# Pace of a woven-in matrix inverse: seven steps instead of six per ten filler calls, then its sixteen transfers at sixteen per ten

## The chip, the cores and the metric

One core of one Trainium2 chip runs the whole kernel. The metric is device microseconds of one execution; lower is better. Five engines matter here: TensorE (PE, with its weight loads PEld), VectorE (DVE), ScalarE (ACT), GpSimd (POOL) and SyncE (SP). Each executes its own list of instructions in order and waits on semaphores of the others. SP, ACT and POOL also issue DMA transfers from their lists.

## The reference

One decoder layer on x of 1024 tokens by 1024 channels, all in fp32:

- h = RMSNorm(x), and one projection P = h W_in whose columns go to three branches and to the branch gates.
- Branch A, RWKV-7 time mixing, 8 heads of 64: a state S (64x64 per head) follows S = S*w + (S(-kk))(kk*a)^T + v k^T over the tokens, and y = S r is normalised per head.
- Branch B, stick-breaking attention, 8 heads of 64: strictly causal, attn = sigmoid(z) times the running product of (1 - sigmoid(z)) between key and query.
- Branch M, attention into 256 memory tokens, 4 heads of 128: softmax(q k^T) v with normalised q and k.
- x += (sum over branches of sigmoid(G_b) * (branch_b W_br[b])) W_out, then x += ConvFFN(RMSNorm(x)).

The recurrence of branch A is computed in chunks of 64 tokens. For 8 heads and 16 chunks that needs the inverses of 128 triangular 64x64 matrices, which are worked out one after the other column, for all 128 at once.

## The kernel before

**Number format.** Every fp32 operand of a large matmul is split into a high and a low part; three matmuls (high-high, low-high, high-low) make one product. For a weight block ACT makes the high part (L80, `wh`) and POOL the low part (L81, `wl`), from a raw tile that SP loads (L76, `wr`). PE (L115) runs the products.

**Stages around the change.** `run` builds one list of *items*, the filler: projections, gate projections (`gate_item`) and the memory keys and values, each a generator that does about an eighth of its matmuls per call. Against this filler, `weave` advances a main generator: first `rwkv_prep` for four head pairs, then the first attention `sb_attn` (64 units), then the second attention `mem_attn` (8 units), then the recurrence `stage2`. After every step of the main generator it calls the filler so many times (1.03 per step in the first attention, 1.6 in the second).

**The inverse.** `inverse` holds the 128 matrices in one tile `inst`, a matrix to a partition. For each of 62 columns it does two DVE instructions over s*(63-s) elements, a product into a scratch tile `it` (L474) and a sum into `inst` (L476). Then the diagonal is set (L478), and sixteen DMAs on POOL's queue (L483) store the result to DRAM as `td`, which `stage2` reads back (L515). Each of the 124 DVE instructions and each of the sixteen transfers is one step. The steps are pulled by the filler: `pumped` adds `pace[0]` to a counter at each call and pulls one step per ten.

```python
def pumped():
    due = 0
    for _ in self.stream(items):
        due += pace[0]
        while due >= 10:
            due -= 10
            next(inv, None)
        yield
```

The pace is zero until the first attention begins. Whatever is left of the inverse is drained ahead of the last gates before `stage2`.

**First attention, one unit:** scores on PE, sigmoid on ACT (L842, into `at`), the running product on DVE (L848, a scan over up to 1024 elements), two units later the transposes on PE (L105), their copy on ACT (L860), and the products with v.

**Second attention, one unit:** `front` makes the scores on PE into `g` banks; DVE takes the row maximum (L1058, `mxt`) and scales it (L1061, `nb`); ACT does four exponentials from the banks (L1064); DVE takes reciprocals and scales (L1068, L1070). Two units later `mid` transposes on PE, and ACT copies out (L1079). Four units later `back` multiplies by v, ACT copies (L1089) and stores (L1090).

**Filler next to it:** a memory query projection ends in `fin` (L1026, L1027 on ACT, L1028 on DVE), which empties its two `mm` banks. A gate projection ends with two copies on ACT (L749), a product on DVE (L750), a sigmoid on ACT (L753) and a store (L755). PSUM has four banks named `mm` and four named `g`; a matmul that starts a bank waits for the reader of what stood there.

**Who sets the order.** Matmuls and instructions marked with `pinned` or `ordered` keep the order in which they are written. For the others (most of ACT, much of DVE, POOL and SP) a scheduler chooses the place from its own estimate of when things are ready, so that a step that is moved changes the order of instructions that it has nothing to do with.

Of the kernel before, what the change touches and what calls it, by code (L numbers as in the profile page):

```python
# [49 lines left out]
class Trunk:  # L50
# [1710 lines left out]
    def run(self):  # L1761
        nc, tc = self.nc, self.tc
        self.setup()
        sx, sw, sl, sr = ExitStack(), ExitStack(), ExitStack(), ExitStack()
        self.pool_x = sx.enter_context(tc.tile_pool(name="xp", bufs=1))
        self.pool_a = sr.enter_context(tc.tile_pool(name="ap", bufs=1, side="right"))
        self.bufs_w = {"w4": 3, "A": 4, "qk": 8, "at": 7, "ys": 1, "it": 1}
        self.pc = [self.pool_a.tile([128, NC], F32, name=f"pc{p}") for p in range(4)]
        self.inst = self.pool_a.tile([128, 64, 64], F32, name="inst", tag="inst")
        self.stored, self.open_gates = set(), []  # L1770
        drain = lambda g: [None for _ in g]
        chain = itertools.chain
        self.pool_w = sw.enter_context(tc.tile_pool(name="w1", bufs=1, side="right"))
        krv, qk, mq = ([[] for _ in range(4)] for _ in range(3))
        krv[0].append(self.startup())
        self.pin = True
        marks, self.fresh = {"k0"}, []
        self.marks = marks
        items = [self.shift_item(i + p, krv[p], f"{n}{p}") for p in range(4) for n, i in (("k", 4), ("r", 0), ("v", 8)) if (p, n) != (0, "k")]
        items += self.sb_v()  # L1780
        self.v = []
        zero = self.t4("ys", n=512)
        nc.vector.memset(zero[0:1], 0.0)
        nc.sync.dma_start(self.vsd[0:1], zero[0:1])
        inv = self.inverse()
        gq = [(b, d) for b in (1, 0) for d in range(8)]
        gq[14:14] = [(2, 0), (2, 1)]
        self.stored = set(gq)
        gate = lambda hook={}: self.gate_item(*gq.pop(0), hook)
        mark = lambda name: lambda: marks.add(name)  # L1790
        for p in range(4):
            kp, kss, qp, hooks = self.sb_qk(p, qk[p])
            items += [*([self.differ] if p == 0 else []), kp, gate({6: self.spread_last} if p == 0 else {}), kss, qp, gate(hooks), mark(f"sb{p}")]
        prep, mss, mv, mk = self.mem_kv()
        mqi = [None] * 4
        for h in range(4):
            mqi[h] = self.mem_q(h, mq[h], {2: mqi[h - 1][1], 4: mark(f"mq{h - 1}")} if h > 1 else {})
        items += [gate({0: prep}), gate(), gate({2: prep}), lambda: mss(0), mv[0], lambda: mss(1), *mv[1:], *mk, mqi[0][0], mark("kv")]
        items += [self.mem_kss, gate({1: mqi[0][1]}), self.mem_kbc, mqi[1][0], mark("mq0")]
        items += [mqi[2][0], mqi[3][0], gate({2: mqi[3][1], 4: mark("mq3")}), gate(), mark("mem")]  # L1800
        ld1, hk1, br1 = self.branch(1, True)
        ld2, hk2, br2 = self.branch(2, False)
        items += [lambda: drain(inv), gate(), ld1, gate(hk1), mark("y1"), *br1, ld2, gate(hk2), *br2, gate()]
        assert not gq
        pace = [0]
# [10 lines that stand above are left out]
        pump = pumped()  # L1816

        def need(name):
            while name not in marks:
                next(pump)  # L1820

        for p in range(4):
            self.weave(self.rwkv_prep(p, krv[p], need), pump, 1.0)
        pace[0] = 6
        need("sb0")
        self.weave(self.sb_attn(qk, need), pump, 1.03, 0)
        need("kv")
        self.weave(self.mem_attn(mq, need), pump, 1.6, 0)
        need("mem")
        st2 = self.stage2()  # L1830
        next(st2)
        need("y1")
        self.weave(st2, pump, 2.15, 0)
        self.weave(self.group_norm(), pump, 1, 0)
        drain(pump)
        self.close_gates()
        self.pin = False
        sx.close()
        self.pool_l = sl.enter_context(tc.tile_pool(name="l4", bufs=16))
        self.branch_last()  # L1840
        sums = self.out_proj()
        self.pool_a.tile([128, 56], F32, name="pad_a")
        sw.close()
        self.bufs_r = {"u": 3, "p1": 2}
        self.pool_r = sr.enter_context(tc.tile_pool(name="ff", bufs=2, side="right", reuse_waits="tile"))
        self.up_phase(*sums)
        self.pool_r.tile([128, 40], F32, name="pad_r", bufs=1)
        self.down_phase()
        sr.close()
        sl.close()  # L1850
# [67 lines left out]
```

## Time and profile before

| what | value |
|---|---|
| time, median of 3 runs | 1827.49 us (1827.40 to 1828.59) |
| the profiled execution's own time | 1825.74 us |
| its span, first to last instruction | 1824.0 us |
| PE busy | 1785.2 us (98%) |
| DVE, ACT, POOL busy | 1182.7, 866.2, 789.8 us |
| first inverse step, last inverse step, last of the sixteen transfers (starts) | 293.9, 687.1, 742.7 us |
| first attention (first scan to last scan) | 332.0 to 626.9 us |

The profile names a tile without its number, and a line can be that of a helper: almost every matmul is L115. A timeline row gives start, duration, engine, line, operation, output<-inputs, size, how many equal instructions are merged, and in brackets the idle time of the engine before it with what ended it. A row of the chain of waits gives start, duration, and engine, tile and line. A windows row gives the stretch, then busy time and number of instructions for each engine, then PEclk (the TensorE clock that was granted, as a share of full speed) and the DMA share.

### The profile page before, as it was taken

The page shows a single profiled execution, that of the slowest core. Times are in us where ns is not written, and L with a number is a line of the kernel's source. Part 1 is how long each engine was busy: PE and PEld are TensorE (multiplying, and loading weights), DVE is VectorE, ACT ScalarE, POOL GpSimd, SP SyncE. Part 2 cuts the span into 40 slices and gives each one's busy share as a digit, 9 for nine tenths or more (in the row PEclk, how much of TensorE's full clock was granted, in tenths as well). Part 3 has the DMA queues.
Part 4 walks back from the last instruction along what each step waited for, and adds up shares of the span by engine and source line. Part 5 has one row for each costly group of instructions (what it writes and reads, how often), then busy time and mean ns, then how long its engine had stood idle before and what let it go on. Part 6 is the DMA issues. An engine that isn't in the chain of part 4 may idle for free.

```text
span 1824.0 us, 27302 instructions
## 1 busy us (share of the span) xinstructions
PE 1785.2 (98%) x10468; PEld 1444.6 (79%) x10468; DVE 1182.7 (65%) x1622; ACT 866.2 (47%) x1553; POOL 789.8 (43%) x447
## 2 busy tenths in 40 slices
PE   8999999999999999899999999989999999999999
PEld 6777778888787887677777878868888888888877
DVE  5667674787888854234542892487776777794595
ACT  5544344556566635434544333554544445444343
POOL 2323353322231433212323541587767777545454
PEclk9999999999999999899999999999999999999999
DMA  4255564211112323468754562322322323395475
GB/s 183 70 163 183 181 218 157 73 41 44 53 56 87 115 92 94 128 236 288 252 181 156 180 233 98 121 86 89 120 98 87 121 93 121 112 347 194 138 259 179
DMA packets 122341, 261.29 MB, mean 143 GB/s; under 512 B 28506, under 2 KB 43098, under 8 KB 122083
## 3 DMA queue, kind: packets, MB, share of 16 engines
q1 hardware_dynamic: 84738, 193.71, 32.3%
q10 hardware_dynamic: 33696, 53.23, 8.0%
q0 software_dynamic: 3776, 12.62, 2.3%
q8 instruction: 82, 1.34, 0.3%
q14 instruction: 49, 0.39, 0.1%
HBM read 178.99 MB, written 80.48 MB: 142 GB/s over the span
## 4 chain that ended last, share of the span: by engine, by line
PE 71%; DVE 3%; issue 3%; ACT 2%; POOL 2%; DMA 2%; SPq 0%; ACTq 0%; POOLq 0%; DVEq 0%
PE mm L115 58%; PE g L115 10%; PE g L105 3%; POOL dw L1657 1%; DVE at L1208 1%; DMA A<-yd 1%; DVE mg L1215 0%; DVE at L1207 0%; DVE w L750 0%; DVE inst L476 0%; DMA u<-in_w_down_dram 0%; DMA mrd<-w 0%; DMA x<-in_x_dram 0%; ACT w L753 0%; DMA wr<-in_w_out_dram 0%
## 5 line engine op out<-in xcount | busy, mean ns | idle before, releaser
L81 POOL TENSOR_TENSOR wl<-wr,wh 128x1024 fp32r<-128x1024 f32 x77 | 198.9, 2584 | 504.0 <-ACT wh L80 504.0
L115 PE MATMUL mm<-xhi,wh 128*128 128x512 f32 x784 | 262.2, 415 | 8.7 <-ACT xhi L185 7.8
L115 PE MATMUL mm<-xlo,wh 128*128 128x512 f32 x784 | 245.1, 394 | 0.9 <-DVE xlo L186 0.9
L115 PE MATMUL mm<-xhi,wl 128*128 128x512 f32 x784 | 243.1, 392 | 0.0
L115 PEld LDWEIGHTS mm<-xlo,wh 128*128 128x128 f32 x784 | 148.1, 189 | 34.7 <-DVE xlo L186 1.6
L115 PEld LDWEIGHTS mm<-xhi,wl 128*128 128x128 f32 x784 | 147.9, 189 | 33.3 <-POOL wl L81 0.5
L115 PEld LDWEIGHTS mm<-xhi,wh 128*128 128x128 f32 x784 | 137.8, 191 | 36.6 <-ACT xhi L185 7.8
L80 ACT ACTIVATE wh<-wr 128x1024 fp32r<-128x1024 f32 x77 | 81.6, 1060 | 145.7 <-PE mm L115 95.9
L115 PE MATMUL mm<-dw,da 128*128 128x512 f32 x528 | 121.2, 390 | 0.4 <-DVE da L1656 0.3
L115 PE MATMUL mm<-BT,l 128*128 128x512 f32 x504 | 117.9, 389 | 1.6 <-POOL l L1386 1.6
L1657 POOL TENSOR_TENSOR dw<-draw,dw 128x512 fp32r<-128x512 f32 x55 | 80.9, 1478 | 83.4 <-ACT dw L1655 83.4
L115 PEld LDWEIGHTS mm<-dw,da 128*128 128x128 f32 x528 | 98.9, 188 | 22.2 <-DVE da L1656 1.1
L848 DVE TENSOR_TENSOR_SCAN at<-at,nrt 128x128 f32<-128x128 f32 (+3 forms) x64 | 88.1, 1386 | 40.3 <-ACT at L842 40.2
L115 PEld LDWEIGHTS mm<-BT,l 128*128 128x128 f32 x504 | 94.5, 188 | 21.6 <-POOL l L1386 2.0
L115 PE MATMUL mm<-BT,wh 128*128 128x512 f32 x352 | 108.8, 390 | 1.6 <-DVE BT L1296 0.9
L115 PE MATMUL mm<-B,wh 128*128 128x512 f32 x352 | 108.5, 389 | 0.0
L1656 DVE TENSOR_TENSOR da<-draw,da 128x512 fp32r<-128x512 f32 x77 | 64.8, 851 | 59.6 <-ACT da L1654 57.1
L115 PE MATMUL g<-dw,da 128*128 128x512 f32 x396 | 92.5, 395 | 2.1 <-POOL dw L1657 1.1
L1386 POOL TENSOR_TENSOR l<-it,l 128x1024 fp32r<-128x1024 f32 x21 | 50.8, 2419 | 92.1 <-ACT l L1383 92.1
L115 PEld LDWEIGHTS g<-dw,da 128*128 128x128 f32 x396 | 75.4, 191 | 18.6 <-POOL dw L1657 1.4
L750 DVE TENSOR_TENSOR w<-w,nrt 128x1024 f32<-128x1024 f32 x24 | 48.8, 2033 | 63.6 <-ACT w L749 52.7
L1654 ACT ACTIVATE da<-draw 128x512 fp32r<-128x512 f32 x77 | 48.3, 629 | 81.5 <-PE mm L115 38.9
(332 smaller groups left out, 3987.1 us busy)
## 6 DMA issues: line engine op xcount, KB each, us to landing
wr<-in_w_in_dram SPq DMA_DIRECT2D x50, 512.0 KB, 3.6
draw<-actd SPq DMA_DIRECT2D x77, 256.0 KB, 3.4
draw<-in_w_down_dram SPq DMA_DIRECT2D x55, 256.0 KB, 4.6
at<-scr SPq DMA_DIRECT2D x24, 512.0 KB, 6.0
wr<-in_w_up_dram SPq DMA_DIRECT2D x22, 512.0 KB, 3.5
actd<-gall ACTq DMA_DIRECT2D x44, 256.0 KB, 3.2
rw<-in_w_up_dram SPq DMA_DIRECT2D x20, 512.0 KB, 3.6
gsd<-w ACTq DMA_DIRECT2D x18, 512.0 KB, 2.8
```

The lines of the kernel that those rows point to most:

```text
L80: self.nc.scalar.activation(hi, raw, AF.Copy)
L81: self.nc.gpsimd.tensor_tensor(lo, raw, hi.bitcast(F32), ALU.subtract)
L105: self.pinned(self.nc.tensor.transpose(out, in_, self.ident[:n, :n]))
L115: self.pinned(self.nc.tensor.matmul(*a, **k))
L750: nc.vector.tensor_tensor(g, g, self.nrb, ALU.mult)
L848: self.pinned(nc.vector.tensor_tensor_scan(sn[:, :W][:, ::-1], sn[:, :W][:, ::-1], self.nrt[:, 1152 - W :][:, ::-1], 1.0, ALU.mult, ALU.max))
L1208: nc.vector.tensor_tensor(g[:, hs], g[:, hs], o[:, hs], ALU.add)
L1386: nc.gpsimd.tensor_tensor(lo, src, hi.bitcast(F32), ALU.subtract)
L1654: self.pinned(nc.scalar.activation(A[:, 0], a, AF.Copy))
L1656: self.pinned(nc.vector.tensor_tensor(A[:, 1], a, A[:, 0].bitcast(F32), ALU.subtract))
L1657: nc.gpsimd.tensor_tensor(Wt[:, 1], w, Wt[:, 0].bitcast(F32), ALU.subtract)
```

## The change

Two lines in `run`, between `rwkv_prep` and `stage2`:

```diff
-        pace[0] = 6
+        pace[0] = 7
         need("sb0")
         self.weave(self.sb_attn(qk, need), pump, 1.03, 0)
         need("kv")
+        pace[0] = 16
         self.weave(self.mem_attn(mq, need), pump, 1.6, 0)
```

So seven steps instead of six are pulled per ten filler calls while the first attention runs, and sixteen per ten from the start of the second. No instruction is added, removed or resized. Buffer numbers aside, PE's list is the same, row for row; the others change in places. Tiles carry numbers in the rows below, and one tile has different numbers in the two kernels.

The first place is ACT in the second attention, where one unit's four exponentials (`at_6282` before, `at_6291` now) and the emptying of a memory query's banks (L1026, L1027) stand. Before:

```order
L1089 ACTIVATE at_6157<-mm_6329 128x512
L1090 DMA yd<-at_6157 128x512
L80 ACTIVATE wh_6365<-wr_6363 128x1024
L1064 ACTIVATE at_6282,sm_6283<-g_6284,nb_6293,hf_6250 128x256 x2
L1079 ACTIVATE at_6334<-g_6335 128x512
L1064 ACTIVATE at_6282,sm_6283<-g_6297,nb_6306,hf_6250 128x256
L1079 ACTIVATE at_6334<-g_6341 128x512
L1026 ACTIVATE qk_6354<-mm_6176,params 128x512
L1027 ACTIVATE w_1136_6353<-mm_6176 128x512
L1026 ACTIVATE qk_6354<-mm_6177,params 128x512
L1027 ACTIVATE w_1136_6353<-mm_6177 128x512
L1064 ACTIVATE at_6282,sm_6283<-g_6297,nb_6306,hf_6250 128x256
```

Now:

```order
L1064 ACTIVATE at_6291,sm_6292<-g_6293,nb_6302,hf_6261 128x256 x2
L1064 ACTIVATE at_6291,sm_6292<-g_6306,nb_6315,hf_6261 128x256 x2
L1089 ACTIVATE at_6169<-mm_6337 128x512
L1079 ACTIVATE at_6342<-g_6343 128x512
L1090 DMA yd<-at_6169 128x512
L1079 ACTIVATE at_6342<-g_6349 128x512
L1026 ACTIVATE qk_6362<-mm_6188,params 128x512
L1027 ACTIVATE w_1136_6361<-mm_6188 128x512
L1026 ACTIVATE qk_6362<-mm_6189,params 128x512
L1027 ACTIVATE w_1136_6361<-mm_6189 128x512
L80 ACTIVATE wh_6372<-wr_6370 128x1024
```

The exponentials have moved ahead of the copy L1089, and the split of a weight block (L80) behind the emptying of the banks.

The second place is ACT two units later, around the end of a gate projection (L749 to L755); the unit's exponentials write `at_6480` before and `at_6484` now. Before:

```order
L1089 ACTIVATE at_6334<-mm_6520 128x512
L1090 DMA yd<-at_6334 128x512
L80 ACTIVATE wh_6592<-wr_6590 128x1024
L749 ACTIVATE w_1174_6551<-mm_6369 128x512
L749 ACTIVATE w_1174_6551<-mm_6370 128x512
L753 ACT_TABLE_LOAD
L753 ACTIVATE w_1174_6551<-w_1174_6551 128x1024
L755 DMA gsd<-w_1174_6551 128x1024
L1064 ACT_TABLE_LOAD
L1064 ACTIVATE at_6480,sm_6481<-g_6482,nb_6491,hf_6461 128x256
L1079 ACTIVATE at_6525<-g_6526 128x512
L1064 ACTIVATE at_6480,sm_6481<-g_6482,nb_6491,hf_6461 128x256
```

Now:

```order
L1064 ACTIVATE at_6484,sm_6485<-g_6486,nb_6495,hf_6467 128x256 x2
L1064 ACTIVATE at_6484,sm_6485<-g_6499,nb_6508,hf_6467 128x256 x2
L1089 ACTIVATE at_6342<-mm_6524 128x512
L1079 ACTIVATE at_6529<-g_6530 128x512
L1090 DMA yd<-at_6342 128x512
L1079 ACTIVATE at_6529<-g_6536 128x512
L80 ACTIVATE wh_6594<-wr_6592 128x1024
L749 ACTIVATE w_1174_6554<-mm_6376 128x512
L749 ACTIVATE w_1174_6554<-mm_6377 128x512
L753 ACT_TABLE_LOAD
L753 ACTIVATE w_1174_6554<-w_1174_6554 128x1024
L1064 ACT_TABLE_LOAD
```

The unit's four exponentials and both copies L1079 now stand ahead of the gate's end. On DVE the same happens: the row L750 of that gate stood ahead of this unit's two rows L1061, and stands behind them now.

The third place is POOL at the end of the first attention. Before, the splits of the memory key weights and of the next blocks follow each other, and the first transfers of `td` come fourteen rows below the first row shown:

```order
L81 TENSOR_TENSOR wl_5452<-wr_5449,wh_5451 128x1024
L81 TENSOR_TENSOR wl_5501<-wr_5498,wh_5500 128x1024
L81 TENSOR_TENSOR wl_5551<-wr_5548,wh_5550 128x1024
L81 TENSOR_TENSOR wl_5606<-wr_5603,wh_5605 128x1024
L81 TENSOR_TENSOR wl_5641<-wr_5638,wh_5640 128x1024
L81 TENSOR_TENSOR wl_5675<-wr_5672,wh_5674 128x1024
```

Now (the first split shown is the same block, `wl_5452` before and `wl_5478` now):

```order
L81 TENSOR_TENSOR wl_5478<-wr_5475,wh_5477 128x1024
L483 DMA td<-inst 8x64x64
L81 TENSOR_TENSOR wl_5527<-wr_5524,wh_5526 128x1024
L81 TENSOR_TENSOR wl_5576<-wr_5573,wh_5575 128x1024
L483 DMA td<-inst 8x64x64
L81 TENSOR_TENSOR wl_5632<-wr_5629,wh_5631 128x1024
L81 TENSOR_TENSOR wl_5668<-wr_5665,wh_5667 128x1024
L483 DMA td<-inst 8x64x64
L81 TENSOR_TENSOR wl_5702<-wr_5699,wh_5701 128x1024
L483 DMA td<-inst 8x64x64 x3
```

The first transfer now stands between the splits of the first and the second memory key block. It waits for the last inverse step on DVE, which now stands nine rows behind the last scan of the first attention (four L474, the diagonal L478, four L476).

## Prediction

> **What bounds the kernel now.** I read the page first, then the table of windows, then PE's rows in the windows where it loses time, then the chain of waits there.
>
> ```profile
> span 1824.0 us, 27302 instructions
> PE 1785.2 (98%) x10468; PEld 1444.6 (79%) x10468; DVE 1182.7 (65%) x1622; ACT 866.2 (47%) x1553; POOL 789.8 (43%) x447
> ```
>
> PE is idle for 1824.0 − 1785.2 = 38.8 us in the whole span. Its list is unchanged by this edit, so there are only two ways to change the time: idle time of PE, and the clock at which it runs. The windows give stretch, then busy time of PE, PEld, DVE, ACT and POOL, then PEclk and the DMA share:
>
> ```profile
> 340.00:640.00 300.00, 297.28 (x2131) 245.79 (x2130) 242.46 (x202) 186.11 (x350) 84.65 (x35) 1.00 0.21 68
> 690.00:740.00 50.00, 45.30 (x278) 35.55 (x276) 17.36 (x46) 22.68 (x56) 17.93 (x19) 0.97 0.42 99
> 740.00:790.00 50.00, 42.94 (x178) 32.74 (x179) 11.75 (x19) 23.27 (x43) 8.76 (x6) 0.90 0.57 187
> 790.00:890.00 100.00, 99.86 (x985) 78.70 (x984) 42.28 (x101) 45.72 (x137) 24.90 (x18) 1.00 0.75 256
> ```
>
> The second attention (690 to 790) is the one stretch that the edit touches where PE loses both: 4.70 + 7.06 = 11.76 us idle, at clocks of 0.97 and 0.90. Three rows of PE's timeline hold all of it (0.41 + 3.18 + 8.17 = 11.76):
>
> ```profile
> 714.61 1.69 PE L115 MATMUL g<-A,qk 128*128 128x256 f32 x12 [0.41 <-ACT at L1064]
> 720.86 2.75 PE L115 MATMUL mm<-at,A 128*128 128x512 f32 x4 [3.18 <-DVE qk L1028]
> 747.06 2.93 PE L115 MATMUL g<-A,qk 128*128 128x256 f32 x12 [8.17 <-ACT at L1079]
> ```
>
> The chain of waits tells what ACT did instead, in the order of its list:
>
> ```profile
> 713.47 1.09 ACT at L1064 x4
> ...
> 738.48 1.06 ACT wh L80
> 739.53 0.98 ACT w L749 x2
> 740.54 2.51 DVE w L750
> ...
> 744.57 1.28 ACT L1064
> ...
> 746.52 0.50 ACT at L1079
> ```
>
> PE finished at 738.9 and wanted a `g` bank. That bank is emptied by L1079, which stands on ACT behind a unit's first exponential, which stands behind the whole gate end: copies, product on DVE, sigmoid, a table load on each side.
>
> **The change part by part.**
>
> *The order in the second attention (gain).* By the first and second order pieces, the unit's exponentials and L1079 stand ahead of the gate's end, and the banks of the memory query are emptied before L80, not after it. What they need is there early. The product L750 has also moved behind two rows L1061; their inputs come from here, so it isn't held:
>
> ```profile
> 731.48 1.41 DVE L1058 TENSOR_REDUCE mxt<-g 128x2 f32<-128x512 f32 x2 [3.28 <-PE g L115]
> 742.96 0.22 DVE L1061 SCALAR_TENSOR_TENSOR nb<-mxt,hf 128x2 f32<-128x2 f32 x2
> 735.30 0.60 ACT L1089 ACTIVATE at<-mm 128x512 f32<-128x512 f32 x1 [9.35 <-PE mm L115]
> ```
>
> The maxima were ready at 732.9, the scale `nb` only at 743.1 because it stood behind L750; ACT had been idle for 9.35 us until 735.3. In the new order the four exponentials run in that gap, and the two L1079 follow their transposes, before PE asks at 738.9. So the 8.17 goes. For the 3.18, PE waited for two `mm` banks emptied by L1026, L1027 and L1028; these now follow the transposes' copies directly, without L80 (1.06) and the exponential (about 0.55) that stood in between, and the exponentials before them had a 7.79 us hole on ACT to run in:
>
> ```profile
> 710.66 0.60 ACT L1089 ACTIVATE at<-mm 128x512 f32<-128x512 f32 x1 [7.79 <-PE mm L115]
> ```
>
> That hole is longer than the four exponentials that start at 713.47 in the chain, so 0.41 and 3.18 go too. Idle time removed: 11.76. I take all of it; the other end is a gain that a later wait takes again (first rival).
>
> *The clock behind the stalls (gain).* The same rows of work stand elsewhere at full clock, start to start:
>
> ```profile
> 725.68 0.62 PE L115 MATMUL mm<-xlo,wh 128*128 128x512 f32 x2
> 708.69 1.88 PE L115 MATMUL mm<-at,A 128*128 128x512 f32 x4
> 711.74 0.63 PE L115 MATMUL mm<-xlo,wh 128*128 128x512 f32 x2
> 752.96 0.62 PE L115 MATMUL mm<-xlo,wh 128*128 128x512 f32 x2
> 704.50 1.60 PE L115 MATMUL g<-A,qk 128*128 128x256 f32 x12
> 707.78 0.62 PE L115 MATMUL mm<-xlo,wh 128*128 128x512 f32 x2
> ```
>
> After the 3.18 stall, 720.86 to 725.68 is 4.82, against 708.69 to 711.74, 3.05: 1.77 lost. After the 8.17 stall, 747.06 to 752.96 is 5.90, against 704.50 to 707.78, 3.28: 2.62 lost. Together 4.39; they go with the stalls. Gain so far 11.76 + 4.39 = 16.15.
>
> The Trainium skill, "TensorE: Matmul & The Clock Gate", Part 1, section on the HAM clock gate, says that PE falls to half rate after an idle window of about 3.4 us and returns after one busy window of that length. By that rule each slow stretch costs half a window, about 1.7, so 3.4 instead of 4.39, an estimate that would make the gain 15.2 and the time 1815.0; the rows, which decide, show more, and the 3.18 gap, below its figure, did cost clock (1.77).
>
> *The POOL queue at the end of the first attention (cost).* By the third order piece, POOL's first transfer stands between the low-part splits of the first and the second memory key block, and waits for the last inverse step, nine DVE rows behind the last scan.
>
> ```profile
> 621.95 7.12 POOL L81 TENSOR_TENSOR wl<-wr,wh 128x1024 fp32r<-128x1024 f32 x2 [2.81 <-ACT wh L80]
> 385.02 1.76 DVE L848 TENSOR_TENSOR_SCAN at<-at,nrt 128x768 f32<-128x768 f32 x1
> 390.78 0.82 PE L105 MATMUL g<-kon,at 128*128 128x128 f32 x6
> 612.07 2.40 POOL L81 TENSOR_TENSOR wl<-wr,wh 128x1024 fp32r<-128x1024 f32 x1
> 621.69 0.80 DVE L476 TENSOR_TENSOR inst<-inst,it 128x650 f32<-128x650 f32 x1
> 622.42 4.47 DVE L848 TENSOR_TENSOR_SCAN at<-at,nrt 128x1024 f32<-128x1024 f32 x1
> 629.86 0.28 PE L115 MATMUL mm<-qk,wl 128*128 128x256 f32 x1
> L476 DVE TENSOR_TENSOR inst<-inst,it 128x236 f32<-128x236 f32 (+2 forms) x3 | 1.0, 342 | 0.1
> L474 DVE TENSOR_TENSOR it<-inst 128x180 f32<-128x180 f32 (+1 forms) x2 | 0.6, 316 | 0.1
> L483 POOL DMA_DIRECT2D td<-inst x16: 798/814/971, 687.7 to 742.7; - x16
> ```
>
> The two splits took 7.12 because DVE's last scan ran beside them (4.47; scan and split ran longer together, as against 2.40 for a split alone, and 1.76 × 1024/768 = 2.3 for a scan by its row at 385.02). Now they come one after the other. The L476 step at 621.69 has passed earlier, so the last scan starts about 621.6: + 2.3 scan, with the first split beside it or behind it + 2.4, + 2.6 for nine small steps (three L476 at 1.0, two L474 at 0.6, the other four about 0.3 each by the same rows, less for the diagonal), + 0.9 for the transfer's issue (814 ns), + 2.4 for the second split: 632.2. PE read the second block's `wl` at 629.86. Stall 2.3. Bounds: 0, if the first split hides behind the scan; 2.9, if scan and split stretch each other by the difference seen; and 1.8 more if the clock falls as it did after the 3.18. I take 2.3 without clock loss, since it is shorter than 3.18, the shortest gap above behind which the clock fell.
>
> Later POOL rows run a few us behind for a while and then have 15 us of transfers out of their way, since 690 to 743 no longer holds them.
>
> *Inverse steps in the first attention (cost).* Seven for six means that DVE carries up to some ten more steps by its end. The step at 621.69 took 0.80 for 650 elements; the widest has 992, so 1.22. DVE was busy for 242.46 of the 300 us from 340 on, 57.5 free, and ten steps of 1.22 are 12.2. One step in a tight place delays a scan by up to 1.2, or about 3 where a split stretches it as the 4.47 was stretched. The tightest scan that I found is the one at 385.02: it ended at 386.78 and PE read it at 390.78, 4.0 later. So 0 is likely; I take 0.3 for a few meetings of two such delays (bounds 0 and 2).
>
> *SP and the rest.* The SP rows that move are loads that `stage2` reads, behind all of this, and from 790 on the lists agree but for numbers. Zero, covered by PE's own work; without that cover the third rival.
>
> *Sum:* −16.15 + 2.3 + 0.3 = −13.5. The profiled execution's own time is 1825.74, 1.74 around its span, giving 1812.2. The median shown, 1827.49, is 1.75 above it; the same step from the median gives 1814.0.
>
> **The rivals.**
>
> *The stall moves on one unit.* The next unit's exponentials still stand behind the gate's end, and the transposes after them want their banks.
>
> ```profile
> 748.46 0.58 ACT L1064 ACTIVATE at<-g,nb,hf 128x256 f32<-128x256 f32 x1
> 762.30 1.04 PE L105 MATMUL g<-kon,at 128*128 128x128 f32 x8
> ```
>
> From 738.9 to the last exponential's end at 749.0 is 10.1; less two copies L1079 (1.1) that now precede, plus a copy L1089 (0.6): 9.6. PE's work from 747.06 to 762.30 is 15.2, less 2.6 of slow clock: 12.6. Margin 3.0. If two further waits of ACT fill it, PE waits for the remainder, 0 to 8.17 with up to 2.62 of clock: 1814 to 1824.8; a middle case, 3.3 + 1.8, is 1819. Against it: only ACT's list sets this, and each row of it is accounted for. Chance 0.08.
>
> *Slower: POOL held for long.* If DVE comes out of the first attention a whole lead behind (ten or eleven steps that found no gap, 11.6 us, and the stretching beside splits, 17 us in all), then the first transfer holds the key blocks' splits for that long, and PE with it: 17 + 2.6 clock against the gain of 16.15 gives about 1831. It decides from an inverse that ends at about 640: at an end of 628.9 (above) the stall is 2.3, at 640 it is 13.4, and with the clock that is the gain. For it: the transfer does stand at the head of the queue. Against it: the 57.5 us that DVE had free. Chance 0.05.
>
> *No change.* What PE gains arrives at 790 to 890 earlier, where the DMA share is 0.75; if those loads bound it, the time is given back: 1827.5. Against it: PE was busy there for 99.86 of 100. Chance 0.03.
>
> **How the numbers follow.** The forecast has 0.84: 1814.0, by its bounds 1811.3 (no cost at all) to 1818.3 (4.7 on POOL, 2 in the first attention). The range reaches 0.8 below and 1.7 above for the partial case of the first rival: 1810.5 to 1820. A measurement of this kernel tells about 0.2% (3.7 us) from no change. Faster by more: 0.84 and 0.07 of the first rival, 0.91; within: its end and the third, 0.03; slower: 0.05 and 0.01 for what I haven't seen, 0.06.
>
> **What would show each step right or wrong.** Right: PE without a wait for L1064, L1028 or L1079 between 690 and 750, and a clock of 1.00 through it; the first `td` transfer issued between 626 and 631; one PE wait for POOL `wl` of about 2 us at 630; 790 to 890 as full as before. Wrong: a PE wait at the transposes after the gate's end (first rival); a `wl` wait over 5 us (second); PE idle after 780 (third); scans that PE or ACT wait for in the first attention by over 2 us.

## The result, and the profile after

The changed kernel takes 1815.5 us (median of 4 runs, 1813.27 to 1817.14) against 1827.45 us before: ratio 0.9933, interval 0.9916 to 0.9951. That is 11.95 us faster; 13.5 had been forecast, and 1814.0. The profiled execution took 1815.64 us.

The page of the changed kernel:

```profile
span 1813.9 us, 27293 instructions
PE 1781.5 (98%) x10468; PEld 1441.8 (79%) x10468; DVE 1178.1 (65%) x1622; ACT 865.0 (48%) x1553; POOL 785.8 (43%) x447
```

The engines' own instructions are as many as before; the nine that are missing of the 27302 are among those that are not counted as busy. Its windows (stretch and its length, then busy time of PE, PEld, DVE, ACT and POOL, then PEclk):

```profile
340.00:640.00 300.00, 293.94 (x2100) 242.08 (x2097) 241.17 (x214) 182.16 (x342) 80.76 (x36) 1.00 0.21 66
690.00:740.00 50.00, 49.88 (x317) 40.70 (x316) 25.17 (x65) 29.48 (x75) 12.04 (x9) 1.00 0.22 70
740.00:790.00 50.00, 50.00 (x228) 38.05 (x227) 17.21 (x21) 25.41 (x39) 7.96 (x5) 1.00 0.64 231
790.00:890.00 100.00, 99.72 (x1047) 78.18 (x1048) 42.83 (x112) 42.84 (x147) 27.48 (x19) 1.00 0.75 262
```

From 690 to 790 PE's idle time has gone from 11.76 us to 0.12, and the clock from 0.97 and 0.90 to 1.00. In return, PE is idle for 6.06 us of 340 to 640, where it was 2.72.

ACT's timeline of the changed kernel at the end of the gate projection, the place of the old 8.17 us wait:

```profile
731.70 0.57 ACT L1064 ACTIVATE at<-g,nb,hf 128x256 f32<-128x256 f32 x1 [5.17 <-DVE nb L1061]
...
733.96 0.60 ACT L1089 ACTIVATE at<-mm 128x512 f32<-128x512 f32 x1
734.45 0.59 ACT L1079 ACTIVATE at<-g 128x512 f32<-128x512 f32 x1
...
734.96 0.60 ACT L1079 ACTIVATE at<-g 128x512 f32<-128x512 f32 x1
...
739.18 1.28 ACT L753 ACT_TABLE_LOAD   x1
```

The exponentials fill ACT's gap ahead of L1089, the two copies L1079 are through by 735.6, and the gate's end with its table load comes behind them. PE asks for the bank at 737.4 and doesn't wait. Two of PE's rows frame the whole place; before, they started at 708.69 and 762.30:

```profile
713.05 1.88 PE L115 MATMUL mm<-at,A 128*128 128x512 f32 x4
...
749.99 1.04 PE L105 MATMUL g<-kon,at 128*128 128x128 f32 x8
```

53.61 us before, 36.94 now: 16.67 gained here, where 16.15 was forecast. The first of the two starts 4.36 later than before: that is the price, and PE's waits from 290 to 800 show 4.0 of it. After:

```profile
PE g L105 <- ACT at L860: 4.0, 3, 3.0
PE mm L115 <- POOL wl L81: 2.4, 2, 1.7
```

Before:

```profile
PE g L105 <- ACT at L860: 2.3, 3, 1.1
```

So 2.4 at the head of POOL's queue, and 4.0 − 2.3 = 1.7 more (1.64 by the single rows) in the first attention. At 749.99 the changed kernel is 12.3 ahead, at its last instruction 10.1: this execution loses 2.2 after 790, in waits that come and go from run to run (PE's wait for L1656 is 0.3 before, 1.4 here and in "the old order back", 0.3 in all other runs). The medians are 11.95 apart all the same, because the profiled execution of the kernel before lies 1.7 below the median of its kernel, and this one at its own.

POOL's rows at the end of the first attention in the changed kernel, and PE's row that waits:

```profile
623.44 3.37 POOL L81 TENSOR_TENSOR wl<-wr,wh 128x1024 fp32r<-128x1024 f32 x1 [3.23 <-ACT wh L80]
629.82 0.91 POOL L483 DMA_DIRECT2D td<-inst  x1 [3.01 <-DVE inst L476]
630.76 4.73 POOL L81 TENSOR_TENSOR wl<-wr,wh 128x1024 fp32r<-128x1024 f32 x2
```

```profile
633.19 0.39 PE L115 MATMUL mm<-qk,wl 128*128 128x256 f32 x1 [1.68 <-POOL wl L81]
641.99 0.39 PE L115 MATMUL mm<-qk,wl 128*128 128x256 f32 x1 [0.70 <-POOL wl L81]
```

POOL stood for 3.01 us with the next split behind a transfer that waited for the last inverse step.

The chain of waits around the first attention's longest wait, changed kernel:

```profile
470.93 2.20 DVE at L848
...
473.16 3.39 DVE qk L811
...
476.57 1.18 DVE inst L476
477.75 1.15 DVE w L750
...
478.92 1.06 ACT w L753
479.98 0.49 ACT at L860
...
480.51 0.66 PE g L105 x4
```

The same place before:

```profile
470.84 1.29 DVE qk L811
...
472.15 3.25 DVE inst L476
475.40 1.15 DVE w L750
476.57 1.06 ACT w L753
```

A gate's product L750 is the last on DVE; ACT's sigmoid L753 waits for it, and the copies L860 that PE wants stand behind the sigmoid. DVE comes to the product 2.35 later than before (477.75 against 475.40). From the copy L264 at 439 on it has done twelve inverse steps instead of ten, and the two more are about that long (1.18 each); since the start of the inverse it has done seventy instead of sixty. So the wait of 1.1 has become 3.0.

### The profile page after: what moved, and what is told of

Its sections match the earlier page's. It is cut to its first block, busy times and chain, and to the rows that moved or that the text cites. A ratio compares the mean times of both kernels' runs of the same rounds, so it can differ in the third digit from the quotient of the medians.

```text
span 1813.9 us, 27293 instructions
## 1 busy us (share of the span) xinstructions
PE 1781.5 (98%) x10468; PEld 1441.8 (79%) x10468; DVE 1178.1 (65%) x1622; ACT 865.0 (48%) x1553; POOL 785.8 (43%) x447
## 4 chain that ended last, share of the span: by engine, by line
PE 67%; DVE 6%; issue 3%; POOL 2%; DMA 2%; ACT 2%; POOLq 0%; ACTq 0%; SPq 0%; DVEq 0%
PE mm L115 55%; PE g L115 9%; PE g L105 3%; DVE at L848 1%; POOL dw L1657 1%; POOL wl L81 1%; DMA wr<-in_w_out_dram 1%; DVE qk L811 1%; DMA A<-yd 1%; DVE inst L476 0%; DVE at L1208 0%; DVE mg L1215 0%; DVE it L474 0%; ACT at L1064 0%; DVE at L1207 0%
## 5 line engine op out<-in xcount | busy, mean ns | idle before, releaser
L81 POOL TENSOR_TENSOR wl<-wr,wh 128x1024 fp32r<-128x1024 f32 x77 | 196.0, 2547 | 493.2 <-ACT wh L80 483.6
L80 ACT ACTIVATE wh<-wr 128x1024 fp32r<-128x1024 f32 x77 | 81.6, 1059 | 145.3 <-PE mm L115 84.0
L1656 DVE TENSOR_TENSOR da<-draw,da 128x512 fp32r<-128x512 f32 x77 | 65.9, 864 | 60.4 <-ACT da L1654 59.8
L750 DVE TENSOR_TENSOR w<-w,nrt 128x1024 f32<-128x1024 f32 x24 | 50.0, 2085 | 56.8 <-ACT w L749 45.9
```

The lines of the kernel that those rows point to most:

```text
L80: self.nc.scalar.activation(hi, raw, AF.Copy)
L81: self.nc.gpsimd.tensor_tensor(lo, raw, hi.bitcast(F32), ALU.subtract)
L750: nc.vector.tensor_tensor(g, g, self.nrb, ALU.mult)
L1656: self.pinned(nc.vector.tensor_tensor(A[:, 1], a, A[:, 0].bitcast(F32), ALU.subtract))
```

## The experiments

The theory: the gain is ACT's order alone, the pace only made the scheduler choose it; the price is an inverse that is late twice, ahead of a gate's product and at the head of POOL's queue. The main rival: the second attention is faster because inverse steps and transfers left its DVE and POOL. Each run is compared with runs of the kernel before on the same chip (their medians 1826.28 to 1828.31).

### Seven alone

```diff
-        pace[0] = 16
```

> The pace of seven in the first attention and no sixteen in the second: the transfers go on at seven per ten calls. ACT's list in the second attention then has the new order of both places, as with the whole change; DVE's list in the first attention is the changed kernel's. Theory (the gain is ACT's order): the three waits of PE between 700 and 750 stay away, 1815 to 1817 us, the whole effect within 1.5 us of the changed kernel. Rival (the gain comes from transfers that leave POOL early, the sixteen): part of the 8.2 us wait comes back, 1820 us or more.

Measured: 1816.66 us, ratio 0.9945 (0.9930 to 0.9961). PE's waits from 290 to 800 are those of the changed kernel (4.0 for L860, 2.3 for L81), none from 690 to 790. The second line of the change adds nothing that can be measured. One thing differs: behind the same wait for L860, 3.04 us here and 3.02 in the changed kernel, the clock fell to 0.66 in this execution:

```profile
480.00:485.00 5.00, 5.00 (x17) 4.15 (x18) 4.89 (x6) 1.63 (x4) 0.00 (x0) 0.66 0.26 105
```

### Sixteen alone

```diff
-        pace[0] = 7
+        pace[0] = 6
```

> Six in the first attention as before, sixteen per ten calls from the start of the second. DVE's list through the first attention and ACT's order at both places stay those of the kernel before; the inverse and its transfers end earlier than before. Theory (order): PE's waits of 0.4, 3.2 and 8.2 us stay, and the time is 1827 us within 1.5. Rival (the second attention got faster because inverse steps and transfers left its DVE and POOL): the waits shrink by at least half, 1820 us or less.

Measured: 1828.16 us, ratio 1.0003 (0.9994 to 1.0011). The old waits are all there:

```profile
PE g L115 <- ACT at L1079: 8.2, 1, 8.2
PE mm L115 <- DVE qk L1028: 3.4, 1, 3.4
```

The last inverse step now starts at 663 instead of 687, and the last transfer at 729 instead of 743: no inverse step is left in the second attention here, and that alone does nothing.

### The old order back

```diff
         nc.vector.memset(X.rearrange("p s t -> p (s t)")[:, 0 : 64 * 64 : 65], 1.0)
+        while "mq1" not in self.marks:
+            yield
```

> The changed kernel, but the sixteen transfers are pulled only once the second memory query is in hand. DVE's list through the first attention is the changed kernel's, row for row, and all inverse steps are done before 630; ACT's order at both places is that of the kernel before (exponentials behind the gate's end, the weight split ahead of the emptying of the banks). Theory (order): the waits of 3.2 and 8.2 us and the slow clock behind them come back on top of the new costs, 1815.5 + 16 = about 1831 us, slower than before. Rival (work that left the second attention): about 1816 us, as the changed kernel.

Measured: 1831.6 us, ratio 1.0019 (1.0009 to 1.0029). PE's rows (this kernel's lines lie two further down):

```profile
724.83 3.68 PE L115 MATMUL mm<-at,A 128*128 128x512 f32 x4 [3.18 <-DVE qk L1030]
750.68 2.93 PE L115 MATMUL g<-A,qk 128*128 128x256 f32 x12 [7.74 <-ACT at L1081]
```

With no inverse step left in the second attention, and no transfer after 710, the waits are back at nearly their old size, and ACT's list is the old one. The rival, which wanted 1816, falls. By this reading it is also what the change would have been without its side effect: a loss.

### The kernel before, pinned

```diff
-                nc.scalar.activation(g[:, h * 512 : (h + 1) * 512], pp[h], AF.Copy)
-            nc.vector.tensor_tensor(g, g, self.nrb, ALU.mult)
+                self.pinned(nc.scalar.activation(g[:, h * 512 : (h + 1) * 512], pp[h], AF.Copy))
+            self.pinned(nc.vector.tensor_tensor(g, g, self.nrb, ALU.mult))
...
-                nc.vector.tensor_reduce(mxt, ...)
+                self.pinned(nc.vector.tensor_reduce(mxt, ...))
...
-                    nc.scalar.activation(e[...], pz[...], AF.Exp, ...)
+                    self.pinned(nc.scalar.activation(e[...], pz[...], AF.Exp, ...))
```

(L1061 likewise.)

> The kernel before, inverse and paces untouched, with the second attention's exponentials and maxima and the gates' copies and products kept in the order in which they are written. ACT then has a unit's first exponentials and both copies L1079 ahead of the gate's end at the second place; the first place stays as before (split ahead of the emptying of the banks). Theory (order): the 8.2 us wait and its 2.6 us of slow clock go, the 3.2 us wait stays, 1827.5 - 10.8 = about 1816.7 us; up to 1821 if a new wait takes part of it, because here only two of the four exponentials precede. Rival (work that left the second attention): no change, 1827 us.

Measured: 1817.93 us, ratio 0.9953 (0.9937 to 0.9968). Most of the effect is there with the inverse untouched:

```profile
720.45 1.98 PE L115 MATMUL mm<-at,A 128*128 128x512 f32 x4 [3.18 <-DVE qk L1028]
738.55 1.70 PE L115 MATMUL g<-A,qk 128*128 128x256 f32 x12 [1.73 <-ACT at L1079]
```

The 8.17 has shrunk to 1.73, since L80 and one exponential still precede the copy; the 3.18 stays, as it should, but here without slow clock behind it (1.00, where it was 0.66).

### The wrong gate

```diff
-        self.nc.gpsimd.tensor_tensor(lo, raw, hi.bitcast(F32), ALU.subtract)
+        low = self.nc.gpsimd.tensor_tensor(lo, raw, hi.bitcast(F32), ALU.subtract)
+        if getattr(self, "late", False):
+            self.pinned(low)
...
         for s in range(1, 63):
             n = 63 - s
+            self.late = s < 40
```

> The changed kernel with POOL's weight splits kept in the order in which they are written until the inverse is at column 40, nothing else. What this moves: at the gate whose product L750 stood behind an inverse step at 477.7, the sigmoid L753 now stands on ACT behind the two copies L860 for which PE waited 3.0 us at 480.5; POOL's splits at three places stand one or two rows later. Theory (the first attention's cost is one gate's product that the inverse delayed, with ACT's copies queued behind its sigmoid): the 3.0 us wait goes and nothing else, 1815.5 - 3.0 = 1812.5 us. Rival (DVE is simply too full there, the scans are late and another wait takes its place): 1815 us or more.

Measured: 1820.4 us, ratio 0.9964 (0.9951 to 0.9977): a miss. PE's row (lines two or three further down):

```profile
483.27 0.66 PE L107 MATMUL g<-kon,at 128*128 128x128 f32 x4 [3.03 <-ACT at L863]
```

The window of its next 5 us, with the granted clock, 0.66, behind POOL's busy time:

```profile
483.00:488.00 5.00, 4.73 (x16) 3.83 (x17) 4.93 (x6) 1.94 (x5) 0.00 (x0) 0.66 0.26 105
```

The wait is still there: the sigmoid that moved belongs to the gate at 436, which nobody waits for. I had read the order and not matched the gate with its time. The kept order of the splits costs PE new waits of 0.57, 0.61 and 0.56 at 333, 368 and 457 (they are in the next run too, which has the same order there, and in no other), and here the clock falls behind the 3.03. The run says nothing on the theory.

### The wrong gate and POOL

```diff
-        self.nc.gpsimd.tensor_tensor(lo, raw, hi.bitcast(F32), ALU.subtract)
+        self.pinned(self.nc.gpsimd.tensor_tensor(lo, raw, hi.bitcast(F32), ALU.subtract))
...
-                    nc.gpsimd.dma_start(self.td[...], X[i0 : i0 + 15 : 2])
+                    self.pinned(nc.gpsimd.dma_start(self.td[...], X[i0 : i0 + 15 : 2]))
```

> The changed kernel with POOL's weight splits and the sixteen transfers both kept in the order in which they are written. The gate's sigmoid stands behind the copies, as in the kernel with the splits alone kept; and no transfer stands between the memory key blocks' splits any more, the first one comes behind the last of them. Theory (head of the queue): PE's waits for a split of 1.7 and 0.7 us at 633 and 642 go as well, another 2.4 us: 1810 us. Rival (the split is late for its own reasons, the raw tile or DVE beside it): as with the splits alone kept, 1812.5 us.

Measured: 1825.14 us, ratio 0.9988 (0.9977 to 0.9998): a miss again. PE's waits for a split are 1.0 and 0.4 us instead of 1.7 and 0.7, though no transfer stands between them. POOL's rows tell what stands there instead:

```profile
639.68 0.53 POOL L493 MEMSET it<- 128x512 f32 x1 [2.77 <-DVE inst L476]
640.17 2.38 POOL L81 TENSOR_TENSOR wl<-wr,wh 128x1024 fp32r<-128x1024 f32 x1
```

A memset that clears a buffer of the scratch tile `it`, written at the start of `stage2` (L493), has come to the head of the queue, and it too waits for the last inverse step: the head of the queue again, with another instruction in it. A new wait of 3.13 us for L860 at 526 comes from another gate's product, behind a copy (L264) that started late, and the clock falls to 0.66 behind it.

### Eight

```diff
-        pace[0] = 7
+        pace[0] = 8
```

> Eight steps per ten calls in the first attention, sixteen in the second. ACT's order in the second attention is that of the changed kernel, so the gain there stays; the inverse ends before the memory keys' splits, whose waits (2.4 us) should go, but POOL's first transfers now stand ahead of other splits. Theory (each step that falls ahead of a gate's product or a scan costs by place, not by DVE's busy share): PE's waits for L860 in the first attention grow by 1 to 4 us over those of seven (4.0 us): 1814 to 1818 us in all. Rival (DVE has room, 57 us free before; the extra steps are hidden): the POOL waits go and nothing is added, 1813 us or less.

Measured: 1823.97 us, ratio 0.9984 (0.9975 to 0.9993), worse than either expectation. The waits for L860 are hardly longer (4.3 us), but other places have come up; the largest is the first scan's, in PE's timeline:

```profile
335.60 0.33 PE L105 MATMUL g<-kon,at 128*128 128x128 f32 x1 [2.08 <-DVE at L848]
```

The window around it, clock 0.68:

```profile
335.00:340.00 5.00, 4.40 (x14) 3.48 (x15) 4.93 (x8) 1.24 (x3) 0.00 (x0) 0.68 0.36 105
```

Two waits for L695 add 1.5, the split at 650 still 1.9, and the clock falls to about two thirds behind three of the waits. That the extra steps are not hidden is shown; that they cost by place fits, but the place that was named is not the one.

### Sigmoids behind the copies

```diff
-                nc.scalar.activation(g, g, AF.Sigmoid, scale=-1.0)
+                self.pinned(nc.scalar.activation(g, g, AF.Sigmoid, scale=-1.0))
...
-                nc.scalar.activation(at[:, w0:w1], pt[:, : w1 - w0], AF.Copy)
+                self.pinned(nc.scalar.activation(at[:, w0:w1], pt[:, : w1 - w0], AF.Copy))
```

> The run before aimed at a gate that costs nothing (at 436) and left the two that do (at 403 and 480) where they were. Here the changed kernel with the gates' sigmoids (L753) and the first attention's copies (L860) kept in the order in which they are written: every sigmoid from 330 to 600 stands behind the copies that follow it now. ACT's order in the second attention and POOL's list are the changed kernel's, but for one row of POOL. Theory (a gate's product late on DVE, with ACT's copies queued behind its sigmoid): PE's waits for L860 of 0.73, 3.02 and 0.23 us go, and with them 4.0 us: 1811.5 us. Rival (DVE's lateness shows elsewhere, at a scan or at a split that waits for ACT): 1814 us or more.

Measured: 1809.99 us, ratio 0.9908 (0.9893 to 0.9923), the fastest of all, 5.5 below the changed kernel's median (4.6 by the two ratios); the two intervals overlap only from 0.9916 to 0.9923. PE's longest waits from 290 to 800:

```profile
PE mm L115 <- POOL wl L81: 0.7, 1, 0.7
PE g L105 <- DVE w L264: 0.2, 1, 0.2
```

ACT's timeline at the gate of the 3.02:

```profile
476.42 1.09 ACT L860 ACTIVATE at<-g 128x512 f32<-128x512 f32 x2
477.81 1.06 ACT L753 ACTIVATE w<-w 128x1024 f32<-128x1024 f32 x1 [0.31 <-DVE w L750]
```

The sigmoid still gets its product at 477.8, but nobody stands behind it: no wait for L860 is left. That part of the price is shown. The wait for a split has shrunk too, from 2.4 to 0.7, which I hadn't expected. POOL still stands 3.02 us behind its first transfer there; why PE loses less by it stays open.

### A faster tail

```diff
             n = 63 - s
+            if s == 46:
+                self.pace[0] = 10
...
-        pace = [0]
+        pace = self.pace = [0]
```

> The changed kernel, with ten steps per ten calls instead of seven from column 46 of the inverse on (the short columns, 782 elements and fewer). The last inverse step then falls some ten units before the first attention's last scan, and the transfers stand two by two between the memory splits without a wait for DVE. ACT's list is the changed kernel's. Theory (POOL waits at the head of its queue for the last inverse step): the waits for a split of 1.7 and 0.7 us at 633 and 642 go, 1815.5 - 2.4 = 1813.1 us. Rival (two transfers of 0.8 us ahead of each split, or the memory norm's rows on POOL behind the first of them, make the splits as late): 1815 us or more.

Measured: 1820.19 us, ratio 0.9965 (0.9953 to 0.9978). The waits at 633 and 642 are gone, with transfers between the splits that no longer wait for DVE, so the head of the queue was their cause. But PE's waits from 560 to 660 are now

```profile
PE g L105 <- ACT at L862: 2.1, 2, 1.9
PE mm L115 <- POOL wl L81: 1.2, 1, 1.2
```

Another gate's product is late (1.9 at 560), and so is a later split (1.2 at 650). Whether the transfers made that split late isn't shown: POOL is idle for 1.65 us just ahead of it, and the high part that it needs (L80) is made at 646.0, when its raw tile has come. The waits alone are only 0.7 more than the changed kernel's. The larger part of the loss is clock, which fell behind both gaps of PE, the one at 480 (2.97) and the one at 560 (1.89):

```profile
480.00:485.00 5.00, 4.40 (x15) 3.52 (x16) 4.90 (x7) 2.27 (x6) 0.00 (x0) 0.66 0.26 105
560.00:565.00 5.00, 5.00 (x18) 4.05 (x17) 3.92 (x8) 3.95 (x9) 0.00 (x0) 0.66 0.26 105
```

Five microseconds at 0.66 are 1.7 lost, twice.

### Both

> Both edits of this call together: sigmoids behind the copies, and the faster tail of the inverse. Theory: both new costs go, 4.0 + 2.4 us: 1809.1 us, which is what removing the stalls of the second attention alone would give less the old kernel's own waits for L860 (2.3). Rival: the two edits compete for ACT and DVE at the end of the first attention and only the larger one counts, 1811.5 us.

Measured: 1811.21 us, ratio 0.9914 (0.9901 to 0.9928). Not 1809: a wait of 1.4 for L860 at 554 and the 1.2 at 642 come with the tail. The rival's number, though the cause is the tail and not a contest of the two edits. No gain over sigmoids behind the copies alone.

### The kernel before, in order

The edits of "the kernel before, pinned" and of "sigmoids behind the copies", on the kernel before.

> The kernel before with its pace of six, and only orders kept as written: the second attention's exponentials and maxima with the gates' copies and products (as in the run of the kernel before, pinned), and now the gates' sigmoids and the first attention's copies as well. No inverse step is pulled earlier. Theory (all that the pace did for the time, it did through ACT's order): the waits of 8.2 and 1.7 us before L1079 go with 2.6 us of slow clock, and the old waits for L860 of 1.1, 1.0 and 0.2 us; the 3.2 us wait for the emptied banks stays: 1827.5 - 8.2 - 2.6 - 2.3 = 1814.4 us, and 1812.6 if the clock does not fall behind the 3.2 us wait. Rival (the inverse's work in the second attention costs time of its own): 1817 us or more, as with the second attention's order alone.

Measured: 1813.19 us, ratio 0.9924 (0.9910 to 0.9938). PE's rows:

```profile
716.63 1.98 PE L115 MATMUL mm<-at,A 128*128 128x512 f32 x4 [3.16 <-DVE qk L1028]
734.77 1.69 PE L115 MATMUL g<-A,qk 128*128 128x256 f32 x12 [1.73 <-ACT at L1079]
```

The window around the first of them, clock 1.00:

```profile
716.00:722.00 6.00, 5.37 (x51) 3.80 (x52) 2.79 (x7) 3.78 (x11) 0.00 (x0) 1.00 0.31 123
```

At the old pace, with orders alone, the time lies in the changed kernel's interval. Even the 3.16 left stands in ACT's list (the first place), not in the inverse.

## Why the prediction was right

**The order in the second attention.** 11.76 forecast, 11.64 measured. "The old order back" and "the kernel before, pinned" show from both sides that it is ACT's order, and not the work that left the stage.

**The clock behind the stalls.** With the idle time 16.15 forecast, 16.67 measured between two rows. The rule of the Trainium skill, "TensorE: Matmul & The Clock Gate", Part 1, would have given 15.2, an estimate; the 16.67 measured is closer to the 16.15 from the rows. But this term is no constant: see the last section.

**POOL's queue.** 2.3 forecast as one wait; it was 1.68, then 0.70 a block later, where the late split had held the raw tile for the next load (PE's chain there leads from the split's end at 633.15 over that load to the next split). The inverse's end was set at 628.9 and came at 629.5. There is luck in both numbers. The last scan kept its 2.26, and what the split held up was one of the small steps behind it, which took 2.51 instead of about 0.4, so that the nine steps took 5.0 and not 2.6, while the 2.4 for the split fell away. And PE came 1.65 late itself, by its waits in the first attention, which hid a part of the second split's lateness (it ended at 633.15, set at 632.2). The clock stayed at 1.00, as chosen, but the reason given, a gap shorter than 3.18, doesn't hold: it fell behind 1.93 at a wait for a split in "eight".

**Inverse steps in the first attention.** This is the term that was mis-sized: 0.3 forecast, 1.64 measured (waits of 0.73, 3.02 and 0.23 against 1.09, 1.02 and 0.23). The step that failed is "The tightest scan that I found is the one at 385.02", from which the term was set near 0: it looked for the lateness at the scans, which had room, and not at the gate's product on the same engine, with PE's copies queued behind its sigmoid on ACT. The three waits for L860 in the profile of before showed that this place had no room. Two more slips are in the working. The ten additional steps are what DVE has by 477; by the last scan of the first attention there are sixteen (116 done at 622, where it was 100). And the upper bound adds up to 1818.0 (1811.3 + 4.7 + 2), not 1818.3. That the clock did not fall behind the 3.02 was luck as well: in "seven alone" it did, at the same place.

**The sum.** −16.67 + 2.38 + 1.64 = −12.65 by the parts, −12.3 by the rows at 749.99, −11.95 by the medians; −13.5 had been forecast. The gain came out 0.5 larger than forecast, the costs 1.4 larger.

**The rivals.** The stall did not move on one unit: from 690 to 790 PE is idle for 0.12 us in all. POOL was not held for long: 3.01, of which PE felt 1.68, and its point of decision, an end of the inverse at 640, was missed by 10 us. The stage right behind gave nothing back: 99.72 of 100 from 790 to 890. The 2.2 that this execution loses come later.

## What to carry to other kernels

Where a scheduler places instructions, a change of pace acts through the order that it happens to provoke: compare the lists first, and look for the instruction that the waiting engine wants and what stands ahead of it in its queue. To price work that is moved on to an engine, take the tightest consumer of every instruction on that engine, not of the one that looks critical, and follow it through the in-order queue behind it. And once the order is known to be the cause, write it down: with a few instructions kept in program order the changed kernel got faster (0.9908 against 0.9933), and the kernel before came level with the changed one (0.9924).

## What the runs showed of the hardware

The clock falls behind some short gaps of PE and not behind equal ones. Behind 3.18 us it fell to 0.66 in the kernel before, and stayed at 1.00 behind the same 3.18 in "the kernel before, pinned" and behind 3.16 in "the kernel before, in order". Behind 3.03 it fell to 0.66 in "the wrong gate" and behind 3.04 in "seven alone", and behind 3.02 at the same place of the changed kernel it did not:

```profile
480.00:485.00 5.00, 4.49 (x22) 3.78 (x23) 4.93 (x6) 2.18 (x5) 0.00 (x0) 1.00 0.26 105
```

Even 1.89 was enough in "a faster tail" and 1.93 in "eight", while 1.68 in the changed kernel was not. So a gap of about 1.9 to 3.2 us costs its length and sometimes about 1.7 more (a third of the next 5 us). The Trainium skill, "TensorE: Matmul & The Clock Gate", Part 1, says that the window that is watched runs free, so that the same kernel meets it at other phases; that agrees with equal gaps that end differently. It also asks for an idle window of about 3.4 us, and there the measurement differs: 1.89 was enough.

DVE and POOL stretch each other: L811 took 3.38 us at 473.16, beside a split on POOL that started at 473.10, and 1.28 alone; the split at 623.44, beside the last scan, took 3.37, and 2.40 alone. The Trainium skill, "SBUF — State Buffer", section on who interferes with whom, says that a DVE instruction with two inputs in SBUF and a POOL instruction that reads SBUF shut each other out, and that the one that comes second waits for the whole of the first. That agrees here: 3.38 is near the split's 2.35 and the 1.28 in a row. Which DVE instruction meets the split is a matter of a microsecond: before, it was the inverse step behind L811 (3.25). At this place it made no difference, as both stand ahead of the product: from the start of L811 to the start of L750 it was 4.56 before and 4.59 now.
